# Six changes of order in a gated two-branch encoder layer on one core

## The chip, the cores and the metric

One core of one Trainium2 chip runs the kernel. The metric is the device time of one execution in microseconds (us); lower is better. The median of three runs before the change is 2126.95 us (2126.74 to 2128.09).

## What is computed

The reference is one pre-norm encoder layer in fp32, applied to two inputs with the same weights: x_sample (512 tokens) and x_prompt (1024 tokens), 1024 features each.

```
xn  = rmsnorm(x)
z   = xn @ W_in          # q_A 512 | k_A 128 | v_A 128 | q_B, k_B, v_B 512 each | gate_A, gate_B 1024 each
A   : grouped-query attention, 8 heads of 64 on 2 key groups; q and k RMS-normalised per head,
      then turned by a 2-D rotary table; softmax over all tokens
B   : neighbourhood attention, 8 heads; a band of rows around each block of 128 queries,
      with a relative position bias
mix = (sigmoid(gate_A) * (o_A @ W_pA) + sigmoid(gate_B) * (o_B @ W_pB)) @ W_out
x   = x + mix
x   = x + relu(rmsnorm(x) @ W_up)^2 @ W_down          # 4096 wide
y   = rmsnorm(x)
```

## The kernel before

**Products.** A fp32 product is three matmuls. Every operand is split into a high part, which ScalarE (ACT) casts to fp32r (`split`, L199 for weights), and a remainder, which VectorE (DVE) computes as operand minus high part (L206); TensorE (PE) adds high x high, low x high and high x low into one PSUM bank (`mm3`, L212). So behind each operand stand an ACT cast and a DVE subtraction, and an operand that comes late mostly comes late by its remainder.

**Trunks and phases.** `run` is called once for each input: trunk 0 is x_sample (names with s0, NB = 1 block of 512 tokens), trunk 1 is x_prompt (s1, NB = 2). A last function does the feed-forward part for both. In a trunk, branch A goes by its two key groups g, each with two phases.

Phase R goes over tiles `tt` of 128 tokens. A tile is projected to q and k (`z`) and v; `chain` (L666) squares the heads (ACT, L672), multiplies by the gains (DVE, L676, `ts`), forms the turned pairs `us` with the sine table (GpSimd, POOL, L685), takes the per-head reciprocal root `rs_A` as a power (POOL, L180, in `rstd`), multiplies by the cosine (DVE, L692), adds the pairs (DVE, L693) and scales into `rr` (ACT, L697). Two tiles later `heads_t` transposes `rr` on PE (`pqs`) and empties the bank into kT and qT: high parts on ACT (L626, L628), remainders on DVE (L629, L631); v goes by L653 and L654. In the first group of trunk 1 the rows of x are normalised on the way: `norm_to` (L294) squares a row on ACT (L296), forms mean and power (`ms_s` L176, L180) and the normalised row `xns` (DVE, L300); `transpose_tile` (L305) transposes it on PE (`ptxs`, L313) and empties the bank into the high part (ACT, L323) and the remainder `xs_1l` (DVE, L329).

Phase A goes over heads and blocks of 128 queries: `s_tile` (L777) computes scores `ss` (L785, L786), row maxima (DVE, L788), exponentials (ACT, L791), reciprocals (DVE, L793) and normalised probabilities `ps` (POOL, L794); PE transposes them (`pTs`, L829), ACT and DVE split them (`pths` L834, `ptls` L835), and PE multiplies by v (L805, L806).

Phase B does the neighbourhood attention in units `i` of one head and one query block: scores `sbs`, bias and softmax (L1059 to L1091), transposes `ptbs` (L1132), their split `bhs` (L1139, L1140; in trunk 1 partly through memory and L1122, L1123), the output `obs`. A head pair's projections `pqbs` and `pkbs` are emptied into qB and kB (remainders L1000 and L1021). Near its end the projection of branch A's output starts (`proj_a`, L889): matmuls `ppas` of the split output `oXs` with the split weights `w_pas`, whose splits wait in the list `oa_held`.

**What sets the order.** A scheduler arranges each engine's queue from the order in which the code is written. `tc.keep_in_program_order(op)` holds an instruction at its written place, `tc.issue_after(ins)` puts what is issued inside it behind `ins`. Work that only has to be done some time is held in a generator queue, `fill`, and its pieces are pulled between the steps: the gates (`gate`, L439) in phases R and A, and `proj_a` at the end of phase B, where `f` (L1201 to L1203) is the number of pieces of three matmuls that a unit pulls. `gate` loads the weights of column chunk c + 1 while it works on chunk c, and holds their splits until the third of eight steps:

```
if k == 2:
    while held:
        held.pop(0)()
```

PSUM is held in two pools, one of two double banks for the scores and one of four single banks, which the gate's products (`gpss`), `pTs`, `ptbs`, `ppas` and others take in turn. A gate bank comes free with the tanh (ACT, L460, `sgs`).

## Time and profile before

| | |
|---|---|
| median of 3 runs | 2126.95 us |
| profiled execution | 2126.34 us |
| its span in the profile | 2124.5 us |
| mean granted TensorE clock | 0.999 |
| busy: PE matmuls / weight loads / DVE / ACT / POOL | 2096.5 / 1839.0 / 1480.0 / 1145.7 / 363.3 us |

The profile lists each instruction with its start from the start of the span, its duration, engine, line, operation and tiles (output <- inputs; buffer numbers are left out). Where an engine was idle before an instruction, brackets give the idle time and the instruction that released it. A PE row can overlap the next, as matmuls are pipelined; the pace is read from start to start. SPq and ACTq are queues that issue transfers.

### The profile page before, as it was taken

The numbers are of one execution on the slowest core, as the hardware profiler recorded it, in microseconds if no ns is written. First come the engines' busy times: TensorE is split into PE (matmuls) and PEld (weight loads), VectorE is DVE, ScalarE is ACT, GpSimd is POOL, SyncE is SP. The second block draws the span as 40 slices with busy tenths as digits, with TensorE's granted clock in tenths as the row PEclk, the third lists the DMA queues.
The fourth block names the chain that finished last, engine by engine and source line by source line (L and its number), as shares of the span: only waits on it lengthen the run. The fifth ranks groups of instructions, "written<-read, shape, count | busy, mean of one in ns | idle before, by whom it ended". The sixth has DMA issues, their size and how long they took to land.

```text
span 2124.5 us, 31728 instructions
## 1 busy us (share of the span) xinstructions
PE 2096.5 (99%) x10871; PEld 1839.0 (87%) x10871; DVE 1480.0 (70%) x2793; ACT 1145.7 (54%) x2487; POOL 363.3 (17%) x446
## 2 busy tenths in 40 slices
PE   9999999999999999999999999999999999999998
PEld 8888778888898888887888999999999988888887
DVE  6666786777647756777873877778777777669563
ACT  6665653666666745556531566666565643334452
POOL 2232310332232314443101100002000000000000
PEclk9999999999999999999999999999999999999999
DMA  6436557530122136876563656568454899688561
GB/s 191 133 99 200 160 150 256 192 86 23 49 70 87 45 84 193 241 224 193 172 227 124 199 181 206 163 230 214 156 162 146 272 350 341 213 280 278 164 204 64
DMA packets 336104, 372.92 MB, mean 176 GB/s; under 512 B 31039, under 2 KB 267207, under 8 KB 335943
## 3 DMA queue, kind: packets, MB, share of 16 engines
q1 hardware_dynamic: 297463, 305.60, 45.6%
q10 hardware_dynamic: 31328, 45.11, 6.2%
q0 software_dynamic: 7152, 20.19, 3.5%
q8 instruction: 86, 1.41, 0.3%
q14 instruction: 75, 0.61, 0.1%
HBM read 274.29 MB, written 97.32 MB: 175 GB/s over the span
## 4 chain that ended last, share of the span: by engine, by line
PE 52%; DVE 1%; issue 0%; ACT 0%; POOLq 0%; POOL 0%; ACTq 0%; DVEq 0%
PE dn L212 20%; PE ua L212 6%; PE ud L212 6%; PE uc L212 6%; PE ops L212 4%; PE ub L212 3%; PE ppbs L212 2%; PE ppas L212 2%; PE dnf L212 2%; PE pt L353 1%; PE obs L212 0%; PE ptbs L1132 0%; ACT pbs L1088 0%; PE sbs L212 0%; DVE A L1458 0%
## 5 line engine op out<-in xcount | busy, mean ns | idle before, releaser
L212 PE MATMUL dn<-wd,ah 128*128 128x512 f32 x1248 | 384.2, 389 | 0.0
L212 PEld LDWEIGHTS dn<-wd,ah 128*128 128x128 f32 x1248 | 234.2, 188 | 48.7
L212 PE MATMUL dn<-wd,al 128*128 128x512 f32 x624 | 242.8, 389 | 0.0
L1457 ACT ACTIVATE ah<-ar 128x512 fp32r<-128x512 f32 x168 | 104.4, 627 | 206.7 <-PE dn L212 185.6
L212 PE MATMUL gpss<-xs_0h,w_gs 128*128 128x512 f32 x512 | 189.4, 402 | 0.8 <-DVE ot_Bs L471 0.4
L1458 DVE TENSOR_TENSOR al<-ar,ah 128x512 fp32r<-128x512 f32 x168 | 114.1, 687 | 76.4 <-ACT ah L1457 66.6
L212 PE MATMUL ud<-B,A 128*128 128x384 f32 x768 | 143.7, 334 | 0.7 <-DVE c L1575 0.7
L212 PE MATMUL uc<-B,A 128*128 128x384 f32 x768 | 143.7, 334 | 0.0
L212 PE MATMUL ua<-B,A 128*128 128x384 f32 x768 | 138.8, 334 | 0.0
L212 PEld LDWEIGHTS dn<-wd,al 128*128 128x128 f32 x624 | 117.1, 188 | 24.2
L794 POOL TENSOR_SCALAR ps<-ps,rls 128x1024 f32<-128x1024 f32 (+1 forms) x96 | 96.8, 1009 | 228.4 <-DVE rls L793 213.8
L212 PEld LDWEIGHTS ud<-B,A 128*128 128x128 f32 x768 | 134.0, 188 | 1.1 <-DVE c L1575 1.1
L212 PEld LDWEIGHTS uc<-B,A 128*128 128x128 f32 x768 | 134.1, 188 | 0.2 <-ACT A L1457 0.2
L834 ACT ACTIVATE pths<-pTs 128x512 fp32r<-128x512 f32 x160 | 94.1, 597 | 73.9 <-PE pTs L829 71.3
L212 PEld LDWEIGHTS ua<-B,A 128*128 128x128 f32 x768 | 133.7, 188 | 0.2
L835 DVE TENSOR_TENSOR ptls<-pTs,pths 128x512 fp32r<-128x512 f32 x160 | 107.5, 686 | 37.7 <-ACT pths L834 36.7
L212 PE MATMUL ops<-wh_os,mgs 128*128 128x512 f32 x384 | 119.4, 390 | 0.0
L788 DVE TENSOR_REDUCE nms<-ss 128x1 f32<-128x1024 f32 (+1 forms) x96 | 99.8, 1040 | 25.0 <-PE ss L786 24.5
L212 PEld LDWEIGHTS gpss<-xs_0h,w_gs 128*128 128x128 f32 x512 | 96.1, 188 | 19.0 <-DVE w_gs L206 0.7
L791 ACT ACTIVATE ps<-ss,nms 128x1024 f32<-128x1024 f32 (+1 forms) x96 | 93.3, 972 | 32.1 <-DVE nms L788 26.2
L180 POOL TENSOR_TENSOR rs_f<-ms_f,mhalf 128x1 f32<-128x1 f32 x6 | 4.0, 667 | 590.7 <-DVE ms_f L176 590.7
L829 PEld LDWEIGHTS pTs<-ident,ps 128*128 128x128 f32 x640 | 78.0, 140 | 28.4 <-POOL ps L794 4.4
(287 smaller groups left out, 5144.2 us busy)
## 6 DMA issues: line engine op xcount, KB each, us to landing
ar<-ud SPq DMA_DIRECT2D x120, 512.0 KB, 5.4
br<-in_w_mlp_down_dram SPq DMA_DIRECT2D x72, 512.0 KB, 5.3
rawu<-in_w_mlp_up_dram SPq DMA_DIRECT2D x64, 512.0 KB, 4.1
ud<-c ACTq DMA_DIRECT2D x128, 192.0 KB, 3.6
raw_gs<-in_w_in_dram SPq DMA_DIRECT2D x32, 512.0 KB, 3.9
ud<-cs SPq DMA_DIRECT2D x64, 192.0 KB
tbs<-pbs SPq DMA_DIRECT2D x24, 384.0 KB, 4.8
bhs<-tbs SPq DMA_DIRECT2D x24, 384.0 KB, 3.7
```

Of the source, the lines that this page charges most:

```text
L180: nc.gpsimd.tensor_tensor(r[:, :n], m[:, :n], mhalf[:, :n], op=ALU.pow)
L212: op = nc.tensor.matmul(out, a, b, **kw)
L353: nc.tensor.transpose(halves[c // 4][:, (c % 4) * P : (c % 4 + 1) * P], t[:, c * P : (c + 1) * P], ident)
L788: nc.vector.tensor_reduce(nm_, s, axis=AX.X, op=ALU.max, negate=True)
L791: op = nc.scalar.activation(p, s, AF.Exp, bias=nm_, accum_out=l)
L794: nc.gpsimd.tensor_scalar(p, p, rl, 1.0, op0=ALU.mult, op1=ALU.mult)
L829: nc.tensor.transpose(pt[:, j * P : (j + 1) * P], PP[u, j][:, kc * P : (kc + 1) * P], ident)
L834: nc.scalar.activation(hi, pt, AF.Copy)
L835: nc.vector.tensor_tensor(lo, pt, hi.bitcast(F32), op=ALU.subtract)
L1457: nc.scalar.activation(hi, src, AF.Copy)
L1458: nc.vector.tensor_tensor(lo, src, hi.bitcast(F32), op=ALU.subtract)
```

## The change

All six edits concern order. The number of instructions on each engine is the same.

- `rstd` gets `pow_pin`, and `chain` uses it: the power of the head norms keeps its written place, behind the two multiplications that form the turned pairs.
- `gate`: for chunks after the group's first (c > c0) the splits of the next chunk's weights are issued behind the last exponential that `s_tile` has issued for the first unit (`last_exp`). This concerns chunks 2 (trunk 0, group 0), 6 and 7 (trunk 0, group 1), 2 and 3 (trunk 1, group 0) and 6 and 7 (trunk 1, group 1).
- `next_norm` keeps the written place of the row norms of tiles 6 and 7 of trunk 1.
- In the first phase R of trunk 1, the norm of tile `tr.ready` is written at tile 0 instead of 1, ahead of the carried transposes, and the next one at tile 1 instead of 2.
- At the end of trunk 0's phase B a unit pulls 3 pieces of `proj_a` instead of 3 or 4.
- In trunk 1's phase B the second pop of `oa_held` in a unit starts one unit later (n - 9 instead of n - 10).

```diff
@@ -171,13 +171,15 @@
     def bias_row(r):
         nc.sync.dma_start(biases[r], shifted[:, :, 7 - r : 23 - r, :])
 
-    def rstd(ss, n, width, name, pin=False):
+    def rstd(ss, n, width, name, pin=False, pow_pin=False):
         m = sml.tile([P, 8], F32, tag="ms", name=f"ms_{name}")
         op = nc.vector.tensor_scalar(m[:, :n], ss, 1.0 / width, EPS, op0=ALU.mult, op1=ALU.add)
         if pin:
             tc.keep_in_program_order(op)
         r = sml.tile([P, 8], F32, tag="rs", name=f"rs_{name}")
-        nc.gpsimd.tensor_tensor(r[:, :n], m[:, :n], mhalf[:, :n], op=ALU.pow)
+        op = nc.gpsimd.tensor_tensor(r[:, :n], m[:, :n], mhalf[:, :n], op=ALU.pow)
+        if pow_pin:
+            tc.keep_in_program_order(op)
         return r
 
     held_pe = []
@@ -428,6 +430,7 @@
         obd = dram.tile([4 * P, T], F32, name=f"obd{N}")
         fill = Fill()
         later_put, slot_no = [], [None]
+        last_exp = []
 
         def put(dst, src):
             if slot_no[0] is None:
@@ -453,8 +456,11 @@
                         if k + 1 < NC8:
                             yield
                         if k == 2:
-                            while held:
-                                held.pop(0)()
+                            with ExitStack() as st:
+                                for ins in last_exp if c > c0 else ():
+                                    st.enter_context(tc.issue_after(ins))
+                                while held:
+                                    held.pop(0)()
                     sg = sgp.tile([P, 512], F32, tag="sg", name=f"sg{nm}", bufs=2)
 
                     nc.scalar.activation(sg, g_, AF.Tanh, scale=0.5)
@@ -612,7 +618,7 @@
 
                 def next_norm(tt):
                     xn = ph.tile([P, D], F32, tag="xn", name=f"xn{N}_{tt}", bufs=2)
-                    xn_of[tt] = norm_to(xn, norm_load(x, tt, ph, f"{N}_{tt}"), gb, f"{N}_{tt}")
+                    xn_of[tt] = norm_to(xn, norm_load(x, tt, ph, f"{N}_{tt}"), gb, f"{N}_{tt}", tt > NT // 2 + 1)
 
                 def heads_t(tt):
                     nm = f"{N}_{g}_{tt}"
@@ -688,7 +694,7 @@
                             S4[:, :, :, e].to_broadcast([P, 5, HD // 2]),
                             op=ALU.mult,
                         )
-                    r = rstd(ss[:, :5], 5, HD, f"A{nm}")
+                    r = rstd(ss[:, :5], 5, HD, f"A{nm}", pow_pin=True)
                     nc.vector.tensor_tensor(t, t, rt[:, 0:1, :].to_broadcast([P, 5, HD]), op=ALU.mult)
                     nc.vector.tensor_tensor(t, t, u, op=ALU.add)
                     rr = pre.pop("rr", None) or ph.tile([P, 6, HD], F32, tag="rr", name=f"rr{nm}", bufs=3)
@@ -746,10 +752,9 @@
                             lag.pop(0)()
                     if fresh and not first:
                         if tt == 0:
+                            xn_of[tr.ready] = norm_to(xn_next, xt, gb, f"{N}_{tr.ready}")
                             tr.p0_t(*tr.carry.pop(0))
                         if tt == 1:
-                            xn_of[tr.ready] = norm_to(xn_next, xt, gb, f"{N}_{tr.ready}")
-                        if tt == 2:
                             next_norm(tr.ready + 1)
                     if first and g == 0 and tt == 1:
                         load_pad()
@@ -810,6 +815,7 @@
 
                 for j in range(4):
                     ends = s_tile(units[0], j)
+                    last_exp[:] = [ends]
                     fill.pull(2)
                 queue = []
                 LAG = 2
@@ -1200,7 +1206,7 @@
                 if i < n - 8:
                     f = (5 if i < 2 else 2 + i % 2) if NB == 1 else 5 - (i % 6 == 5)
                 else:
-                    f = 3 + i % 2 if NB == 1 else 8
+                    f = 3 if NB == 1 else 8
                 if NB == 2 and i == n - 11:
                     pa = proj_a(ph, raw_here)
                     next(pa)
@@ -1255,7 +1261,7 @@
                 fill.pull(f - f // 2)
                 for u in due_v.get(i, ()):
                     v_unit(u)
-                if NB == 2 and oa_held and i >= n - 10:
+                if NB == 2 and oa_held and i >= n - 9:
                     oa_held.pop(0)()
                 while later_put and later_put[0][0] < i:
                     nc.sync.dma_start(*later_put.pop(0)[1:])
```

The order of instructions on the engines shows what this moves. Line numbers after the change are 2 to 6 higher than before; names end in the tile's running number.

First, DVE where trunk 0 ends phase R of group 1 (values `vts`, keys `kTs` and queries `qTs` of tile 3, row maxima `nms` and reciprocals `rls` of the first block, `w_gs0_2304_7` the gate weights of chunk 7). Before:

```order
L654 TENSOR_TENSOR vts0_1_3_1624<-zvs0_1_3_1599,vts0_1_3_1624 128x4x64
L206 TENSOR_TENSOR w_gs0_2304_7_1829<-raw_gs0_2304_7_0_1827,w_gs0_2304_7_1829 128x512 x2
L629 TENSOR_TENSOR kTs0_1_1259<-pqs0_1_3_1641,kTs0_1_1259 128x128
L631 TENSOR_TENSOR qTs0_1_0_1257<-pqs0_1_3_1641,qTs0_1_0_1257 64x2x128
L631 TENSOR_TENSOR qTs0_1_1_1258<-pqs0_1_3_1641,qTs0_1_1_1258 64x2x128
L788 TENSOR_REDUCE nms0_1_0_0_0_1671<-ss0_1_0_0_0_1668 128x1
```

After:

```order
L660 TENSOR_TENSOR vts0_1_3_1624<-zvs0_1_3_1599,vts0_1_3_1624 128x4x64
L635 TENSOR_TENSOR kTs0_1_1259<-pqs0_1_3_1641,kTs0_1_1259 128x128
L637 TENSOR_TENSOR qTs0_1_0_1257<-pqs0_1_3_1641,qTs0_1_0_1257 64x2x128
L637 TENSOR_TENSOR qTs0_1_1_1258<-pqs0_1_3_1641,qTs0_1_1_1258 64x2x128
L793 TENSOR_REDUCE nms0_1_0_0_0_1671<-ss0_1_0_0_0_1668 128x1
L798 RECIPROCAL rls0_1_0_0_0_1676<-ls0_1_0_0_0_1674 128x1
L793 TENSOR_REDUCE nms0_1_0_0_1_1691<-ss0_1_0_0_1_1688 128x1
L798 RECIPROCAL rls0_1_0_0_1_1696<-ls0_1_0_0_1_1694 128x1
L793 TENSOR_REDUCE nms0_1_0_0_2_1712<-ss0_1_0_0_2_1709 128x1
L798 RECIPROCAL rls0_1_0_0_2_1717<-ls0_1_0_0_2_1715 128x1
L793 TENSOR_REDUCE nms0_1_0_0_3_1732<-ss0_1_0_0_3_1729 128x1
L208 TENSOR_TENSOR w_gs0_2304_6_1701<-raw_gs0_2304_6_0_1699,w_gs0_2304_6_1701 128x512 x2
```

The two remainders of chunk 7 no longer stand between the values and the keys of tile 3. Those of chunk 6 stand behind the fourth row maximum, those of chunk 7 still further behind.

Second, ACT at the start of phase A of group 1 in trunk 1 (exponentials `ps`, split probabilities `pths`, the gate's tanh `sgs`). Before:

```order
L791 ACTIVATE ps1_1_0_0_3_7890,ls1_1_0_0_3_7891<-ss1_1_0_0_3_7883,nms1_1_0_0_3_7888 128x1024
L791 ACTIVATE ps1_1_0_1_0_7918,ls1_1_0_1_0_7919<-ss1_1_0_1_0_7911,nms1_1_0_1_0_7916 128x1024
L834 ACTIVATE pths1_1_0_0_0_7907<-pTs1_1_0_0_0_7902 128x512
L834 ACTIVATE pths1_1_0_0_1_7932<-pTs1_1_0_0_1_7927 128x512
L460 ACTIVATE sgs1_2304_4_1_7952<-gpss1_2304_4_1_7857 128x512
L791 ACTIVATE ps1_1_0_1_1_7943,ls1_1_0_1_1_7944<-ss1_1_0_1_1_7936,nms1_1_0_1_1_7941 128x1024
```

After:

```order
L796 ACTIVATE ps1_1_0_0_3_7890,ls1_1_0_0_3_7891<-ss1_1_0_0_3_7883,nms1_1_0_0_3_7888 128x1024
L201 ACTIVATE w_gs1_2304_6_7966<-raw_gs1_2304_6_0_7964 128x1024
L201 ACTIVATE w_gs1_2304_7_8426<-raw_gs1_2304_7_0_8424 128x1024
L840 ACTIVATE pths1_1_0_0_0_7907<-pTs1_1_0_0_0_7902 128x512
L796 ACTIVATE ps1_1_0_1_0_7918,ls1_1_0_1_0_7919<-ss1_1_0_1_0_7911,nms1_1_0_1_0_7916 128x1024
L840 ACTIVATE pths1_1_0_0_1_7932<-pTs1_1_0_0_1_7927 128x512
L466 ACTIVATE sgs1_2304_4_1_7952<-gpss1_2304_4_1_7857 128x512
```

Two casts of gate weights, which were made in phase R before, now stand between the fourth exponential of the first block and the first split of its probabilities.

Third, DVE late in phase B of trunk 1 (remainders of attention output `oXs`, projection weights `w_pas`, queries `qBs` and keys `kBs` of the last head pair; L1059, L1100 and L1090 belong to the softmax of a unit). Before:

```order
L206 TENSOR_TENSOR oXs1_0_1_11016<-rawos1_0_1_11014,oXs1_0_1_11016 128x512 x2
L1000 SCALAR_TENSOR_TENSOR qBs1_3_11110<-pqbs1_3_1_11250,qBs1_3_11110 64x128 x4
L1123 TENSOR_TENSOR bhs1_5_2_11211<-bhs1_5_2_11211 128x768
L206 TENSOR_TENSOR w_pas1_0_11010<-raw_pas1_0_0_11008,w_pas1_0_11010 128x256 x2
L1059 ISA sbss1_5_3_0_11222,nmbs1_5_3_0_11223<-sbs1_5_3_11213,bms1_5_3_0_11214 128x384
L1059 ISA nmbs1_5_3_0_11223 128x1
L1059 ISA sbss1_5_3_1_11225,nmbs1_5_3_1_11226<-sbs1_5_3_11213,bms1_5_3_1_11218 128x384
L1059 ISA nmbs1_5_3_1_11226 128x1
L1100 STREAM_TRANSPOSE pbs1_5_0_11098<-pbs1_5_0_11098 128x768
L1090 RECIPROCAL rlbs1_5_3_0_11234<-lbs1_5_3_0_11232 128x1
L1090 RECIPROCAL rlbs1_5_3_1_11239<-lbs1_5_3_1_11237 128x1
L1021 TENSOR_TENSOR kBs1_3_0_11111<-pkbs1_3_1_11285,kBs1_3_0_11111 64x512 x2
```

After:

```order
L1027 TENSOR_TENSOR kBs1_3_1_11112<-pkbs1_3_0_11158,kBs1_3_1_11112 64x512
L208 TENSOR_TENSOR oXs1_0_0_11013<-rawos1_0_0_11011,oXs1_0_0_11013 128x512 x2
L1129 TENSOR_TENSOR bhs1_5_2_11206<-bhs1_5_2_11206 128x768
L1006 SCALAR_TENSOR_TENSOR qBs1_3_11110<-pqbs1_3_1_11245,qBs1_3_11110 64x128 x8
L1027 TENSOR_TENSOR kBs1_3_0_11111<-pkbs1_3_1_11280,kBs1_3_0_11111 64x512 x2
L208 TENSOR_TENSOR w_pas1_0_11010<-raw_pas1_0_0_11008,w_pas1_0_11010 128x256 x2
L208 TENSOR_TENSOR oXs1_0_1_11016<-rawos1_0_1_11014,oXs1_0_1_11016 128x512
L1027 TENSOR_TENSOR kBs1_3_1_11112<-pkbs1_3_1_11280,kBs1_3_1_11112 64x512
L477 TENSOR_TENSOR ot_Bs1_4_3_11338<-obs1_4_3_11331,ot_Bs1_4_3_11338 64x512
```

The keys now follow the queries, ahead of the projection weights and of the second piece of attention output; the softmax rows have moved up, out of this stretch.

## The prediction

> **What bounds the kernel now.** The page comes first. Its first part gives the busy time of each engine, share of the span and number of instructions.
>
> ```profile
> span 2124.5 us, 31728 instructions
> ...
> PE 2096.5 (99%) x10871; PEld 1839.0 (87%) x10871; DVE 1480.0 (70%) x2793; ACT 1145.7 (54%) x2487; POOL 363.3 (17%) x446
> ```
>
> TensorE (PE) works through 2096.5 of 2124.5 us. The change takes no instruction away, so all that it can win lies in the other 28.0 us: the moments in which PE has reached a matmul whose operand or PSUM bank isn't ready. The profiled execution took 2126.34 us, 1.84 more than its span and 0.61 less than the median of 2126.95; I sum against the profiled one and add the result to the median. The second view is the list of waits of PE, each row a matmul that waited, the instruction that released it, the sum, the count and the longest.
>
> ```profile
> PE sbs L212 <- DVE kBs L1021: 2.6, 2, 2.1
> PE zs L212 <- DVE xs_1l L329: 1.5, 1, 1.5
> ...
> PE ss L786 <- DVE kTs L629: 1.3, 2, 1.0
> ...
> PE obs L212 <- DVE bhs L1140: 1.1, 1, 1.1
> PE pTs L829 <- POOL ps L794: 0.8, 3, 0.3
> ...
> PE ptxs L313 <- DVE ms_s L176: 0.5, 1, 0.5
> PE ptxs L313 <- DVE xns L300: 0.5, 1, 0.5
> ```
>
> The reader should see single events, not a rate: one wait for remainders of neighbourhood keys, one for x remainders, two for transposed keys, one for turned-back probabilities. Each of the six edits passes one of these places. How much one costs is read from start to start in the timeline of PE, here where trunk 0 goes from phase R to phase A of group 1.
>
> ```profile
> 128.40 0.39 PE L212 MATMUL gpss<-xs_0l,w_gs 128*128 128x512 f32 x1
> 128.62 0.39 PE L212 MATMUL gpss<-xs_0h,w_gs 128*128 128x512 f32 x1
> 129.45 0.50 PE L785 MATMUL ss<-kTs,qTs 128*128 128x512 f32 x1 [0.44 <-DVE vts L654]
> 130.91 0.50 PE L786 MATMUL ss<-kTs,qTs 128*128 128x512 f32 x1 [0.96 <-DVE kTs L629]
> ```
>
> Undisturbed, one 128x512 matmul follows another after 0.22 to 0.23 us (128.40 to 128.62). The two score matmuls start 0.83 and 1.46 us after the one before, so they lose 0.60 and 1.23, while the listed waits are 0.44 and 0.96: an interruption costs some 0.16 to 0.27 more than the idle time in brackets, because the pipeline fills again. I add 0.17 to every wait that vanishes.
>
> **Gate weights, trunk 0.** VectorE (DVE) at the same place:
>
> ```profile
> 129.37 1.28 DVE L206 TENSOR_TENSOR w_gs<-raw_gs,w_gs 128x512 fp32r<-128x512 f32 x2
> 130.57 0.28 DVE L629 TENSOR_TENSOR kTs<-pqs,kTs 128x128 fp32r<-128x128 f32 x1
> ```
>
> The last key remainder stands behind two remainders of gate weights, 1.28 us, which nobody needs for a long time. The changed order takes both away (the first pair of rows from the order), and with them the remainder of the chunk before, a few rows ahead. The key remainder then ends not at 130.85 but 1.28 + 0.64 sooner, at about 128.9, when PE would ask for it at 129.08, and the value remainder ahead of it comes sooner too. Gain 0.60 + 1.23 = 1.8. The splits return between the first exponentials and their row sums, where I charge 0.2.
>
> **Gate weights, trunk 1.** In group 0 the second of the two kTs waits (1.3 - 0.96 = 0.34, with the refill 0.5) goes in the same way; group 1 has no such wait. But both groups pay. These are ScalarE (ACT) behind the fourth exponential of group 1, the mean of one cast of gate weights, and PE at the same moment:
>
> ```profile
> 655.82 0.19 ACT L791 ACTIVATION_READ_ACCUMULATOR ps<-ss,nms 128x1 f32 x1
> 657.36 1.11 ACT L791 ACTIVATE ps<-ss,nms 128x1024 f32<-128x1024 f32 x1 [1.35 <-DVE nms L788]
> ...
> 658.47 1.07 ACT L834 ACTIVATE pths<-pTs 128x512 fp32r<-128x512 f32 x2
> 659.42 0.61 ACT L460 ACTIVATE sgs<-gpss 128x512 f32<-128x512 f32 x1
> ```
>
> ```profile
> L199 ACT ACTIVATE w_gs<-raw_gs 128x1024 fp32r<-128x1024 f32 x32 | 33.6, 1063 | 4.1 <-DMA raw_gs<-in_w_in_dram 2.5 <-issue 1.4
> ```
>
> ```profile
> 659.23 0.60 PE L829 MATMUL pTs<-ident,ps 128*128 128x128 f32 x4
> ...
> 660.35 0.40 PE L212 MATMUL gpss<-xs_0h,w_gs 128*128 128x512 f32 x1
> ```
>
> Two casts (2 x 1.06 = 2.1 at most, 2.0 with the overlap) now fill the 1.35 us of idle time from 656.0 and end near 658.0. Two pths casts (0.95 from start to start of the tanh), an exponential (1.1) and then the tanh that empties the gate's bank follow in ACT's queue: the tanh starts near 660.05 instead of 659.42 and ends near 660.65. The next gate matmul needs that bank. It started at 660.35, behind three score matmuls (3 x 0.23 = 0.69) that the new order of PE puts after it: PE asks at about 659.66. New wait 660.65 - 659.66, about 0.9 to 1.0; I take 0.9 in each group. Bounds: 0, if the exponential's own input comes late enough that nothing is in front of the tanh, and both casts in full, 2.1, in each group. I take 0.9 as the rows around it give every term of it. Net for trunk 1: -0.5 + 1.8 = +1.3.
>
> **Norms one tile sooner, powers behind turned pairs.** DVE and GpSimd (POOL) in phase R of trunk 1:
>
> ```profile
> 407.29 1.28 DVE L300 SCALAR_TENSOR_TENSOR xns<-xts,rs_s,gbs 128x1024 f32<-128x1024 f32 x1 [1.16 <-POOL rs_s L180]
> ...
> 408.90 1.28 DVE L329 TENSOR_TENSOR xs_1l<-ptxs,xs_1h 128x512 fp32r<-128x512 f32 x2
> ...
> 413.84 0.49 DVE L676 TENSOR_TENSOR ts<-zs,gtab 128x320 f32<-128x320 f32 x1
> ...
> 416.21 0.49 DVE L692 TENSOR_TENSOR ts<-ts,rts 128x320 f32<-128x320 f32 x1 [1.75 <-POOL us L685]
> ```
>
> ```profile
> 413.88 1.18 POOL L180 TENSOR_TENSOR rs_As<-ms_As,mhalf 128x5 f32<-128x5 f32 x1 [3.01 <-DVE ms_As L176]
> 415.02 1.16 POOL L685 TENSOR_TENSOR us<-ts,rts 128x160 f32<-128x160 f32 x2
> ```
>
> Up to 408.5 DVE is held by a row norm (1.16 idle for its power, then 1.28 of work) that belongs to the tile after the one PE waits for: the 1.5 us wait for xs_1l. With both row norms asked for one tile sooner this norm is done before, and tile 4's own (the 0.5 wait on xns) is too. The 0.5 wait listed under ms_s is for a PSUM bank that the x remainders free; they stand behind L692 at 416.21, which waits for the turned pairs, which wait for a power of 1.18 us. With the power behind them the pairs can start when L676 ends, near 414.33, and L692 some 0.7 us sooner at the least. The power is needed only after the sum behind L692, so it moves into cover. Gain 1.5 + 0.5 + 0.5 + 3 x 0.17 = 3.0, of which I leave 0.3 because a 128x1024 norm step of 1.28 us now lies in tiles 0 and 1 instead: 2.7. Pinning the norms of tiles 6 and 7 and the powers of trunk 0 I cost at nothing; PE shows no wait there that ends on them.
>
> **Key remainders ahead of projection weights.** PE and DVE late in phase B of trunk 1:
>
> ```profile
> 975.19 0.34 PE L212 MATMUL sbs<-kBs,qBs 128*128 128x384 f32 x1
> 977.65 0.81 PE L212 MATMUL sbs<-kBs,qBs 128*128 128x384 f32 x3 [2.12 <-DVE kBs L1021]
> ...
> 986.62 0.39 PE L212 MATMUL ppas<-oXs,w_pas 128*128 128x512 f32 x1
> ```
>
> ```profile
> 973.09 0.76 DVE L206 TENSOR_TENSOR w_pas<-raw_pas,w_pas 128x256 fp32r<-128x256 f32 x2 [1.57 <-ACT w_pas L199]
> ...
> 976.23 1.36 DVE L1021 TENSOR_TENSOR kBs<-pkbs,kBs 64x512 fp32r<-64x512 f32 x2
> ```
>
> DVE sits idle for 1.57 us for a cast of projection weights that nothing needs before 986.62, works it off, passes a softmax tile, and only then writes the keys that PE asked for at 975.37. In the new order the keys stand ahead of the weights and the softmax tile before both. Put at 973.09 or sooner, the pair of 1.36 ends by 974.45, 0.9 before PE asks. Gain 2.12 + 0.17 = 2.3. The weights and the attention output that are moved back have from 976 to 986.62; that is the cover, and beyond it their delay would be a wait one to one.
>
> **Fewer fillers per unit at the end of trunk 0's phase B.** PE and DVE:
>
> ```profile
> 309.68 0.38 PE L1132 MATMUL ptbs<-ident,pbs 128*128 128x128 f32 x2
> 309.81 0.48 PE L212 MATMUL obs<-bhs,vss 128*128 128x256 f32 x2
> ```
>
> ```profile
> 310.92 0.42 DVE L1140 TENSOR_TENSOR bhs<-ptbs,bhs 128x256 fp32r<-128x256 f32 x1
> ```
>
> The last transposes start at 309.68 and their remainder is there at 311.34, 1.66 us on; only one pair of matmuls lies between, so the last output matmul waits the listed 1.1. The new order leaves nine projection matmuls (9 x 0.23 = 2.0) between these transposes and that pair and nine more behind it, so 1.66 is covered. Gain 1.1 + 0.17 = 1.3. Every transpose moves up too, by at most fifteen matmuls (3.4 us); if its probabilities were not ready then, that much could come back, but no row of the list shows PE waiting for them near here. The load of the next projection weights moves behind two other loads on the SP queue; its cover is the rest of the phase.
>
> **A rule against the change.** The gate remainders read two SBUF operands, and they move to where POOL normalises the probabilities:
>
> ```profile
> 470.64 0.67 DVE L206 TENSOR_TENSOR wgls<-rawqs,wghs 128x512 fp32r<-128x512 f32 x1
> ```
>
> ```profile
> 470.81 1.49 POOL L794 TENSOR_SCALAR ps<-ps,rls 128x1024 f32<-128x1024 f32 x1 [0.70 <-DVE rls L793]
> ```
>
> ```profile
> L794 POOL TENSOR_SCALAR ps<-ps,rls x96: 691/1120/1508, 54.7 to 759.0; 128x1024 f32<-128x1024 f32 x64, 128x512 f32<-128x512 f32 x32
> ```
>
> The last row has shortest, median and longest in ns; 64 of the 96 are of this size. A normaliser that starts 0.50 us before such a remainder ends took 1.49, 0.37 over the median. The Trainium skill (SBUF — State Buffer, section "SBUF: two separate sides") says that VectorE, when it reads two SBUF inputs, and GpSimd lock a shared port pair for a whole instruction, and the later one blocks; the trace agrees, with 0.37 of the 0.50. By that rule the sum would be the second rival below.
>
> **The sum.** -1.8 + 0.2 (trunk 0) + 1.3 (trunk 1, gates) - 2.7 - 2.3 - 1.3 = -6.6. On the profiled time that is 2119.7, on the median 2120.3. The likeliest case's own range: without any of the new waits -8.9 (with the 0.3 back), so 2118.0; with 2.1 instead of 0.9 in both groups -4.2, so 2122.7.
>
> **Rivals.** A measurement of this kernel tells about 0.2%, 4.25 us, from no change, so up to 2122.7 is faster.
>
> First, waits handed on: the queue is as long as before, and the next instruction is late instead. The norm step of 1.28 then holds up a tile's eviction in tile 0 or 1, giving the 1.67 of the xs_1l wait back, and the displaced projection weights reach 986.62 late and give back the 2.3. That is -6.6 + 1.67 + 2.3 = -2.6, 2124.3: no change. For it: ACT and DVE lose no work. Against: both have idle time around these places (1.16 and 1.57 in the rows).
>
> Second, the port: each of the 14 moved remainders (three chunks in trunk 0, four in trunk 1, two each) meets a normaliser: 14 x 0.37 = 5.2, thus -1.4, 2125.5. Against it, three waits of PE on the normaliser sum to 0.8 in the whole list, so they are mostly covered.
>
> Third, slower: phase A runs at the pace of the chain from reduction through exponential and normaliser to transposes, and what is put into it lengthens it one to one. Seven casts at 1.06 and 14 remainders at 0.64 (half of 1.28) are 7.4 + 9.0 = 16.4 in place of the 2.0 charged: -6.6 - 2.0 + 16.4 = +7.8, 2134.8. It decides from the point where ACT or DVE has no room left. Phase A of group 1 in trunk 1, with length and busy time of PE, PEld, DVE, ACT and POOL:
>
> ```profile
> 655.00:700.00 45.00, 44.91 (x246) 36.81 (x246) 32.71 (x53) 32.20 (x57) 16.00 (x14) 1.00 0.11 32
> ```
>
> Against: 12 of 45 us are free on both, and two casts and four remainders need 2.1 and 2.6.
>
> **Chances.** The forecast 0.78; handed on 0.11; port 0.06; slower 0.05. So faster 0.78, same 0.17, slower 0.05. The time is 2120.3. The range takes in the likeliest case and the first rival: 2117.6, a little under its lower end as 0.17 per interruption may be 0.2, to 2124.4.
>
> **What would show it.** Right: the rows kBs L1021 (its 2.1), xs_1l, bhs L1140 and both kTs leave the list of PE's waits, and new ones on the tanh (sgs L460 in the old numbers) of some 0.7 appear at the starts of phase A in trunk 1. Wrong: new rows on oXs or w_pas near 985, on normalised probabilities in phase A, on qTs or kTs in tiles 0 to 2 of trunk 1, or more transposes of ptbs waiting before 310. If PE's busy time or clock changes, the argument is about the wrong thing.

## The result and the profile after

The changed kernel takes 2116.49 us (2115.74 to 2118.62, 6 runs), the kernel before on the same chip 2126.82 us (6 runs): ratio 0.9952, 95% interval 0.9939 to 0.9965, so 10.3 us less (7.4 to 13.0). The forecast was 6.6 less, and its range ended at 2117.6, 1.1 us short of what came. That margin is small: timed again (below, "The change again") the same program took 2118.26 us, 8.7 less than before (6.4 to 11.7), which lies inside the range. So what was wrong is read from the single stretches rather than from the total. The profiled execution took 2116.56 us. The first lines of its page, to be held against those of before:

```profile
span 2114.6 us, 31728 instructions
...
PE 2092.2 (99%) x10871; PEld 1838.6 (87%) x10871; DVE 1478.7 (70%) x2793; ACT 1146.4 (54%) x2487; POOL 361.8 (17%) x446
```

The same instructions, the same work on DVE, ACT and POOL: what is gone is waiting. PE's busy time fell as well, by 4.3 of the 9.9 us by which the span is shorter, which the prediction had named as a sign of being wrong. Here it isn't one: the matmuls are the same and the mean granted clock is 0.999 in both, but a matmul behind an interruption is recorded as longer (0.50 us at 130.91 before, 0.39 now), and 1.0 of the 4.3 is the start of the kernel, which no edit touches. The list of waits of PE in the changed kernel, the rows that answer to those of before (columns: matmul and line, releaser, sum, count, longest; lines are those of the changed kernel, 2 to 10 higher):

```profile
PE zs L214 <- DVE xs_1l L331: 1.2, 1, 1.2
PE ppas L214 <- DVE ot_Bs L477: 1.1, 1, 1.1
...
PE ppbs L214 <- ACT oXs L485: 0.5, 1, 0.5
PE sbs L214 <- DVE kBs L1027: 0.5, 1, 0.5
...
PE pTs L835 <- POOL ps L799: 0.3, 1, 0.3
...
PE pTs L835 <- DVE ptls L841: 0.2, 1, 0.2
```

The long wait for kBs (2.1) and those for kTs, bhs, tile 4's xns and the bank behind ms_s have left the list, as forecast. The wait for xs_1l has not: 1.2 of 1.5 is still there. Two rows of some size are new: ppas behind ot_Bs, 1.1, and ppbs behind oXs, 0.5. No row on the tanh (sgs) stands at a start of phase A; the forecast wanted one in each group of trunk 1. The place that the prediction read first, PE at the start of phase A of trunk 0's second group, now looks so:

```profile
126.54 0.39 PE L214 MATMUL gpss<-xs_0h,w_gs 128*128 128x512 f32 x1
126.77 0.39 PE L790 MATMUL ss<-kTs,qTs 128*128 128x512 f32 x1
126.99 0.39 PE L791 MATMUL ss<-kTs,qTs 128*128 128x512 f32 x1
```

0.22 to 0.23 us from start to start: both interruptions are gone.

**Where the time went.** Every kernel here issues the same 10871 matmuls, so the time between the starts of two of them, counted in order of start, compares one stretch of work across kernels (inside a stretch the order of the products can differ). The columns are single profiled executions: before, after, the changed program profiled a second time (again), and three kernels that have one part of the change each (described below).

| matmuls | what lies there | before | after | again | gates | powers | norms |
|---|---|---|---|---|---|---|---|
| 0 to 50 | start of the kernel | 12.22 | 11.35 | 12.22 | 11.78 | 11.42 | 11.35 |
| 200 to 700 | trunk 0, group 0, R to A | 85.54 | 84.79 | 84.77 | 84.75 | 85.13 | 85.53 |
| 700 to 825 | trunk 0, group 1, R to A | 27.77 | 25.11 | 25.11 | 25.11 | 26.11 | 27.72 |
| 1475 to 1640 | trunk 0, end of phase B | 34.36 | 33.43 | 33.66 | 34.40 | 34.31 | 34.31 |
| 1990 to 2050 | trunk 1, tiles 0 and 1 | 9.12 | 8.47 | 8.45 | 10.12 | 8.44 | 8.73 |
| 2050 to 2150 | trunk 1, xs_1l | 16.13 | 15.62 | 15.02 | 15.89 | 17.67 | 17.75 |
| 2150 to 2390 | trunk 1, group 0, R to A | 35.88 | 34.94 | 34.93 | 34.94 | 34.94 | 35.14 |
| 2390 to 2530 | start of phase A, group 0 | 28.27 | 27.56 | 27.56 | 27.55 | 28.25 | 28.27 |
| 3550 to 3650 | start of phase A, group 1 | 18.67 | 18.66 | 18.65 | 18.68 | 18.65 | 18.65 |
| 5000 to 5250 | keys in trunk 1's phase B | 55.24 | 53.51 | 53.50 | 55.82 | 54.95 | 54.93 |

After less before: -0.87, -0.75, -2.66, -0.93, -0.65, -0.51, -0.94, -0.71, -0.01 and -1.73, together -9.76 of the 9.9 by which the span is shorter. The first of these is none of the change's: no edit touches the start, and the same program took 12.22 there the second time. Three of the entries are marked by the clock and not by an edit: 55.82 (gates), 17.67 (powers) and 17.75 (norms) each hold 3.41 us at half the granted clock; see the norms alone.

### The profile page after: what moved, and what is told of

Same layout as the page of the kernel before. It is cut to its first block, busy times and chain, and to the rows that moved or that the text cites. A ratio compares the mean times of both kernels' runs of the same rounds, so it can differ in the third digit from the quotient of the medians.

```text
span 2114.6 us, 31728 instructions
## 1 busy us (share of the span) xinstructions
PE 2092.2 (99%) x10871; PEld 1838.6 (87%) x10871; DVE 1478.7 (70%) x2793; ACT 1146.4 (54%) x2487; POOL 361.8 (17%) x446
## 4 chain that ended last, share of the span: by engine, by line
PE 78%; DVE 1%; issue 1%; ACT 0%; POOL 0%; DMA 0%; POOLq 0%; DVEq 0%; ACTq 0%
PE dn L214 20%; PE gpss L214 8%; PE ud L214 6%; PE ua L214 6%; PE uc L214 6%; PE ops L214 3%; PE ub L214 3%; PE pTs L835 3%; PE zs L214 2%; PE ppbs L214 2%; PE pqbs L214 2%; PE pkbs L214 2%; PE ppas L214 2%; PE zvs L214 2%; PE dnf L214 2%; PE os L811 1%
## 5 line engine op out<-in xcount | busy, mean ns | idle before, releaser
L799 POOL TENSOR_SCALAR ps<-ps,rls 128x1024 f32<-128x1024 f32 (+1 forms) x96 | 97.4, 1016 | 227.6 <-DVE rls L798 209.6
```

The source lines that it names most:

```text
L799: nc.gpsimd.tensor_scalar(p, p, rl, 1.0, op0=ALU.mult, op1=ALU.mult)
```

## The experiments

Each kernel was timed beside the kernel before on the same chip.

**One part of the change alone: the gates.** The kernel before with this edit (and `last_exp`, which it needs):

```diff
                         if k == 2:
-                            while held:
-                                held.pop(0)()
+                            with ExitStack() as st:
+                                for ins in last_exp if c > c0 else ():
+                                    st.enter_context(tc.issue_after(ins))
+                                while held:
+                                    held.pop(0)()
```

> The kernel before with the edit of the gate weights alone. Theory now: the splits cost PE nothing where they return, because the gate's next products don't take the bank that the delayed tanh empties; the gains at the ends of phase R stay: about -0.4 and -2.2 in trunk 0, -1.0 to -1.6 in trunk 1, together about -4, near 2123. Rival, the step of the prediction: a new wait of 0.9 at the start of phase A in each group of trunk 1, so -1.6 + 1.3 = -0.3, near 2126.5.

Measured: 2121.53 us (2120.01 to 2124.46, 11 runs) beside 2126.67, ratio 0.9975 (0.9966 to 0.9984), 5.1 us less. All of trunk 0's gain ahead of phase B is there (-0.79 and -2.66), trunk 1's start of phase A is 0.72 shorter in group 0 and unchanged in group 1. So the edit that was charged +1.3 in trunk 1 costs nothing there.

**All but the gates.** The changed kernel with the lines above undone:

```diff
-                            with ExitStack() as st:
-                                for ins in last_exp if c > c0 else ():
-                                    st.enter_context(tc.issue_after(ins))
-                                while held:
-                                    held.pop(0)()
+                            while held:
+                                held.pop(0)()
```

> All edits but that of the gate weights. Theory now: the rest of the change is worth what is left of it, about -6, near 2121, in the stages where its edits act, and the stalls at the ends of phase R (group 1 of trunk 0, group 0 of trunk 1) are back with 1.8 and 0.7 us. Rival: the gates are worth next to nothing, as the prediction's sum has it, and this kernel runs like the whole change, near 2117.

Measured: 2121.15 us (2119.16 to 2121.81, 7 runs), ratio 0.9972 (0.9961 to 0.9983), 5.5 us less than before. Its stretch 700 to 825 takes 26.15 and 2150 to 2390 takes 34.91: something other than the gates removes 1.6 of the first and all of the second. The 0.7 at the start of phase A of group 0 is the gates' own: without them 2390 to 2530 takes 28.23.

**The powers alone.** The kernel before with

```diff
-                    r = rstd(ss[:, :5], 5, HD, f"A{nm}")
+                    r = rstd(ss[:, :5], 5, HD, f"A{nm}", pow_pin=True)
```

> The kernel before with the power of the head norms in its written place alone. Theory: the 0.7 us at the transposes of tile 6 in phase R of trunk 1 go, and in trunk 0 some 0.4 us at the heads of group 1: -0.5 to -1.2, near 2126. Rival: a power that waits behind the pairs makes the scaled heads late, 0.5 us or more slower.

Measured: 2123.08 us (2122.22 to 2123.91, 10 runs) beside 2127.3, ratio 0.9982 (0.9973 to 0.9991), 4.2 us less, several times what was expected. PE and DVE of this kernel in trunk 0, group 1:

```profile
127.97 0.50 PE L788 MATMUL ss<-kTs,qTs 128*128 128x512 f32 x1 [0.47 <-DVE kTs L631]
```

```profile
126.09 0.42 DVE L656 TENSOR_TENSOR vts<-zvs,vts 128x256 fp32r<-128x256 f32 x1
126.43 1.28 DVE L208 TENSOR_TENSOR w_gs<-raw_gs,w_gs 128x512 fp32r<-128x512 f32 x2
127.63 0.28 DVE L631 TENSOR_TENSOR kTs<-pqs,kTs 128x128 fp32r<-128x128 f32 x1
```

The gate remainders still stand in front of the last keys. But the turned pairs no longer stand behind a power on GpSimd, so DVE is through the tiles ahead sooner and comes to these rows sooner: its sum (L693 before, L695 here) for the last tile starts at 121.51 instead of 124.44, 2.9 us sooner, while PE is only 1.3 us ahead there. The wait of 0.96 is 0.47 and that of 0.44 is gone. The powers of trunk 0, costed at nothing, are worth 1.66 and 0.41 there. In trunk 1 they take away the same 0.94 from 2150 to 2390 as the gates do, and the wait of 0.54 for the bank behind ms_s; but the norm still stands in front of the remainder of x, and the wait for xs_1l is 2.19 us instead of 1.5.

**The norms alone.** The kernel before with

```diff
                         if tt == 0:
+                            xn_of[tr.ready] = norm_to(xn_next, xt, gb, f"{N}_{tr.ready}")
                             tr.p0_t(*tr.carry.pop(0))
                         if tt == 1:
-                            xn_of[tr.ready] = norm_to(xn_next, xt, gb, f"{N}_{tr.ready}")
-                        if tt == 2:
                             next_norm(tr.ready + 1)
```

and the pinned norms of tiles 6 and 7.

> The kernel before with the two edits of the row norms alone (one tile sooner, tiles 6 and 7 in their written place). Theory now: the row norm of tile 4 now asks for its x row when the load has hardly landed, and the remainders of tile 4 still stand behind the product with the cosine, so most of the 2.3 us expected does not come: 0 to -1.0, 2125.7 to 2126.7, with waits of ScalarE on the x row and a wait of PE of about 1.3 for the remainders left. Rival, the prediction's step: both waits go, -2.0, near 2124.7.

Measured: 2126.28 us (2125.61 to 2127.52, 10 runs), ratio 0.9997 (0.9988 to 1.0006): nothing that stands clear of the noise. The norm is out of the way, and the remainder now stands behind the product with the cosine, which waits for the pairs; DVE and PE of this kernel:

```profile
408.15 0.49 DVE L692 TENSOR_TENSOR ts<-ts,rts 128x320 f32<-128x320 f32 x1 [1.80 <-POOL us L685]
408.56 0.68 DVE L329 TENSOR_TENSOR xs_1l<-ptxs,xs_1h 128x512 fp32r<-128x512 f32 x1
```

```profile
409.30 0.44 PE L212 MATMUL zs<-wghs,xs_1l 128*128 128x384 f32 x1 [2.20 <-DVE xs_1l L329]
```

With powers or norms alone the stretch 2050 to 2150 is 1.5 to 1.6 longer than before (17.67, 17.75), more than the stretch ahead of it gains (0.4 to 0.7); with both it is 0.5 to 1.1 shorter. The wait itself is only 0.7 longer than before (2.19 and 2.20 against 1.50). The rest is the clock: in both profiles the granted clock of TensorE falls to 0.50 for 3.41 us, 0.8 to 0.9 us behind the end of this wait: from 407.44 us with the powers alone and from 410.12 with the norms alone. The first row gives a window of the kernel with the powers alone (us), its length, PE's busy time and matmuls, the granted clock, and the DMA engines' share and GB/s; the others are PE in it:

```profile
407.50:410.80 3.30, 3.30 (x15) 0.50 0.33 122
```

```profile
409.16 0.52 PE L214 MATMUL zs<-wghs,xs_1h 128*128 128x384 f32 x1
409.48 0.52 PE L214 MATMUL zs<-wgls,xs_1h 128*128 128x384 f32 x1
```

These products start 0.32 us apart, and 0.17 to 0.18 at full clock. Half of 3.41 us, some 1.7, is lost (an estimate); without that both stretches would be near 16.0, as long as before, as the 0.7 lost at xs_1l is won back at the bank behind ms_s. In the changed kernel the longest of these waits is 1.19, and its profile shows no such stretch of half clock. The profile of the gates alone has one too, from 974.78 us behind a wait of 1.84 for kBs. It doesn't follow every time: the kernel before waits 2.12 for kBs, and the one with the cosine behind the remainders 2.02 for a bank, at full clock. What decides, and how many of the other executions have it, no trace here shows.

**The two edits of phase B alone.** The kernel before with

```diff
-                    f = 3 + i % 2 if NB == 1 else 8
+                    f = 3 if NB == 1 else 8
...
-                if NB == 2 and oa_held and i >= n - 10:
+                if NB == 2 and oa_held and i >= n - 9:
```

> The kernel before with the two edits of phase B alone (3 pieces per unit in trunk 0, second pop one unit later in trunk 1). Theory: -0.9 at the end of trunk 0's phase B, where the first product with branch B's output now waits 0.5 to 0.65 us for its last piece, and -1.7 in trunk 1, where 2.4 us go and up to 0.9 come back because the remainders of the second projection weights run beside the bias masks on GpSimd (0.8 and 1.1 us instead of 0.42 each): -2.6, near 2124.1. Rival, the prediction's steps: -3.6, near 2123.1, with neither of the new waits.

Measured: 2124.22 us (2123.46 to 2125.42, 10 runs), ratio 0.9988 (0.9979 to 0.9997), 3.1 us less; 53.52 for 5000 to 5250 and 33.90 for 1475 to 1640. The four parts alone are worth 5.1 + 4.2 + 1.0 + 3.1 = 13.4, all together 10.3 or, in the next run, 8.7: they overlap. The table shows where: from 700 to 825 gates and powers take away 2.66 and 1.66 alone and 2.66 together, and from 2150 to 2390 gates, powers and norms take away 0.94, 0.94 and 0.74 alone and 0.94 together.

**The change again**, the same program, for the spread of a profile.

> The whole change once more, unaltered, beside the next two kernels. If its time is a property of the program: 2116.5 within 1 us again, with the first 50 matmuls over after 11.4 us and matmuls 1990 to 2050 in 8.5. If the two places drift from execution to execution, as the 11.35 to 12.2 and 8.4 to 10.3 of the other kernels allow: up to 2118.5, with either place longer.

Measured: 2118.26 us (2117.40 to 2119.89, 5 runs) beside 2126.97, ratio 0.9958 (0.9945 to 0.9970), 8.7 us less. Over both, 11 runs from 2115.74 to 2119.89. The stretches of the table agree within 0.1 us but for the start (12.22 against 11.35), 1475 to 1640 (33.66 against 33.43) and 2050 to 2150 (15.02 against 15.62).

**The tanh later still.** The changed kernel with four casts of 128x512, into a tile that nothing reads, behind the fourth exponential in both groups of trunk 1, to see how much room ACT has before a late tanh costs something:

```diff
                     last_exp[:] = [ends]
+                    if NB == 2 and j == 3:
+                        idle = ph.tile([P, 512], F32, tag="idle", name=f"idle{N}_{g}", bufs=1)
+                        for _ in range(4):
+                            tc.keep_in_program_order(nc.scalar.activation(idle, xh(0, 0), AF.Copy))
                     fill.pull(2)
```

> The whole change, with four casts of 128x512 more (0.5 us each, into a buffer that nobody reads) on ScalarE behind the fourth exponential of each group of trunk 1, so that the tanh starts 2 us or more later than in the whole change. Theory: ScalarE has only about 0.2 us left there, and PE waits 1 to 2 us in each group at the first matmul that takes the tanh's bank or the probabilities behind it, not at the gate's products: +2 to +4 us, near 2119.5. Rival: ScalarE has room for all of it, no new wait of PE over 0.3, near 2116.5.

Measured: 2118.17 us (2117.98 to 2118.95, 4 runs), ratio 0.9960 (0.9947 to 0.9974), as without the casts; the starts of phase A take 27.60 and 18.66 us. First ACT and PE of the changed kernel at the start of phase A of group 1:

```profile
647.82 0.19 ACT L796 ACTIVATION_READ_ACCUMULATOR ps<-ss,nms 128x1 f32 x1
647.91 1.99 ACT L201 ACTIVATE w_gs<-raw_gs 128x1024 fp32r<-128x1024 f32 x2
...
651.97 0.61 ACT L466 ACTIVATE sgs<-gpss 128x512 f32<-128x512 f32 x1
```

```profile
651.22 0.60 PE L835 MATMUL pTs<-ident,ps 128*128 128x128 f32 x4
651.58 0.47 PE L214 MATMUL gpss<-xs_0h,w_gs 128*128 128x512 f32 x1
```

Then the same of the kernel with the casts:

```profile
649.25 0.19 ACT L796 ACTIVATION_READ_ACCUMULATOR ps<-ss,nms 128x1 f32 x1
...
655.53 0.61 ACT L466 ACTIVATE sgs<-gpss 128x512 f32<-128x512 f32 x1
```

```profile
652.65 0.60 PE L839 MATMUL pTs<-ident,ps 128*128 128x128 f32 x4
653.00 0.48 PE L214 MATMUL gpss<-xs_0h,w_gs 128*128 128x512 f32 x1
```

The tanh now starts 6.28 us after the row sum of the fourth exponential (649.25 to 655.53) instead of 4.15 (647.82 to 651.97), and the next chunk's first gate matmul starts 2.53 us ahead of it. So that matmul does not need the bank which the tanh empties. The theory that 0.2 us of room was left falls; ACT has more than 2 us. The trace of the kernel before had it already, if not at the place that the prediction read: of the 47 times that one gate product follows another, the next one starts ahead of the tanh that empties the last one's bank in 21. One of them lies 11 us ahead of that place (PE and ACT of the kernel before):

```profile
648.82 0.39 PE L212 MATMUL gpss<-xs_1h,w_gs 128*128 128x512 f32 x1
```

```profile
649.11 0.59 ACT L460 ACTIVATE sgs<-gpss 128x512 f32<-128x512 f32 x1
```

**The cosine apart.** The changed kernel, in which VectorE needn't wait for the pairs before the product, as this goes into another tile:

```diff
-                    nc.vector.tensor_tensor(t, t, rt[:, 0:1, :].to_broadcast([P, 5, HD]), op=ALU.mult)
-                    nc.vector.tensor_tensor(t, t, u, op=ALU.add)
                     rr = pre.pop("rr", None) or ph.tile([P, 6, HD], F32, tag="rr", name=f"rr{nm}", bufs=3)
+                    tc_ = rr[:, :5, :]
+                    nc.vector.tensor_tensor(tc_, t, rt[:, 0:1, :].to_broadcast([P, 5, HD]), op=ALU.mult)
+                    nc.vector.tensor_tensor(t, tc_, u, op=ALU.add)
```

> The whole change, and the product with the cosine is written into the buffer that the scaled heads take later, not over its own input. Theory: the x remainders that PE still waits 1.2 us for in phase R of trunk 1 stand on VectorE behind that product, and it waits for GpSimd only because it overwrites what GpSimd reads; with another buffer the wait shrinks to 0.3 or less and the time falls by 1 to 1.5 us, near 2115.3. Rival: the remainders are late by their own cast on ScalarE or by the row norm, the wait stays at 1.2 and the time at 2116.5.

Measured: 2118.37 us (2117.71 to 2119.17, 5 runs), ratio 0.9961 (0.9948 to 0.9973). PE of this kernel:

```profile
404.19 0.44 PE L214 MATMUL zs<-wghs,xs_1l 128*128 128x384 f32 x1 [0.61 <-DVE xs_1l L331]
405.81 1.06 PE L315 MATMUL ptxs<-ident,xns 128*128 128x128 f32 x8 [1.00 <-DVE ms_s L176]
```

The wait for xs_1l goes from 1.19 to 0.61, and 1.00 appears at the transposes of the next tile, which wait for the bank that the second remainder frees (by the order on DVE; the row names ms_s, right behind it). 15.58 us for the stretch against 15.62: handed on.

**The cosine behind the remainders.** The changed kernel with that product (and what hangs on it) written, and held, behind the x remainders, for tile 2 of trunk 1 alone:

```diff
+                    def rest(pin=False):
-                    nc.vector.tensor_tensor(t, t, rt[:, 0:1, :].to_broadcast([P, 5, HD]), op=ALU.mult)
+                        op = nc.vector.tensor_tensor(t, t, rt[:, 0:1, :].to_broadcast([P, 5, HD]), op=ALU.mult)
+                        if pin:
+                            tc.keep_in_program_order(op)
...
+                    if fresh and not first and tt == NT // 2 - 2:
+                        rests.append(rest)
+                    else:
+                        rest()
...
                         next_tile()
+                        while rests:
+                            rests.pop(0)(True)
```

> The changed kernel, with the product of tile 2's heads with the cosine (and the sum and scaling behind it) written behind the x remainders of tile 4 in the first phase R of trunk 1, and held there. Nothing else moves on VectorE, and the first transposes of tile 5 stand five matmuls sooner on TensorE. My theory: the 1.19 us wait for xs_1l that the change left behind is there only because the remainder stands behind a product that waits 1.20 us for GpSimd's turned pairs. With the remainder ahead, both are done 0.7 us after their casts, near 402.4 on the clock of the profiled run, and the wait goes (1.19 and 0.17 of refill); tile 5's transposes then ask near 401.9 for the bank that the second remainder frees near 402.4, and give back some 0.5 to 0.7. So the stretch of 100 matmuls goes from 15.6 us to 14.8 or 15.0, and the whole to 0.7 us under the changed kernel's, 2116 to 2117.5. Rival, waits handed on: VectorE then stands still for the power of tile 6's norm, whose own queue place on GpSimd is behind the same turned pairs, the product of tile 2 comes 2 us later, and the turned heads of tile 2 or the values behind it keep TensorE waiting: the stretch stays at 15.6 or more, or the stretch behind it grows beyond 34.94 by as much. Second rival: what an undisturbed run shows there is the landing of the rows, and the stretch in front grows by what this one loses.

Measured: 2119.74 us (2117.30 to 2122.35, 6 runs) beside 2126.61, ratio 0.9967 (0.9954 to 0.9979). First DVE and PE of the changed kernel:

```profile
402.29 0.49 DVE L698 TENSOR_TENSOR ts<-ts,rts 128x320 f32<-128x320 f32 x1 [1.20 <-POOL us L691]
402.70 0.68 DVE L331 TENSOR_TENSOR xs_1l<-ptxs,xs_1h 128x512 fp32r<-128x512 f32 x1
```

```profile
403.43 0.44 PE L214 MATMUL zs<-wghs,xs_1l 128*128 128x384 f32 x1 [1.19 <-DVE xs_1l L331]
```

Then DVE and PE of this kernel:

```profile
401.75 1.28 DVE L331 TENSOR_TENSOR xs_1l<-ptxs,xs_1h 128x512 fp32r<-128x512 f32 x2
402.95 0.14 DVE L176 TENSOR_SCALAR ms_s<-sss 128x1 f32<-128x1 f32 x1
404.69 1.29 DVE L302 SCALAR_TENSOR_TENSOR xns<-xts,rs_s,gbs 128x1024 f32<-128x1024 f32 x1 [1.60 <-POOL rs_s L180]
405.89 0.49 DVE L699 TENSOR_TENSOR ts<-ts,rts 128x320 f32<-128x320 f32 x1
...
409.19 0.17 DVE L176 TENSOR_SCALAR ms_As<-ssAs 128x5 f32<-128x5 f32 x1 [1.00 <-ACT sqs L678]
```

```profile
413.46 1.06 PE L315 MATMUL ptxs<-ident,xns 128*128 128x128 f32 x8 [2.02 <-DVE ms_s L176]
```

The remainders follow one another with no idle time ahead of them, and the wait for xs_1l is gone, as the theory had it. But the product comes 4.14 us after the first remainder starts (401.75 to 405.89) instead of ahead of it, ACT's scaling and then its squares of the next tile come late with it (the 1.00 before ms_As), and the transposes of tile 6 wait 2.02 for a bank. The stretch takes 15.71: the rival was right, and the whole wait turned up one tile later. (This profile also took 271.22 us between matmuls 3650 and 5000, late in phase B, against 268.97 in the changed kernel's; the edit doesn't touch that.)

**The x row loaded first.** The changed kernel with the row of x for tile 4 issued on SP ahead of the first gate weights and the gains:

```diff
-            nxt_w = load_cols(win, goff + c0 * P, P, f"g{N}_{goff}_{c0}")
+            with ExitStack() as st:
+                for ins in x_load if goff == 2304 and c0 == 0 else ():
+                    st.enter_context(tc.issue_after(ins))
+                nxt_w = load_cols(win, goff + c0 * P, P, f"g{N}_{goff}_{c0}")
...
+                    xt = ph.tile([P, D], F32, tag="xt", name=f"xt{N}_{tr.ready}", bufs=2)
+                    x_load.append(nc.sync.dma_start(xt, x[tr.ready * P : (tr.ready + 1) * P, :]).ins)
                     gb = ph.tile([P, 1, D], F32, tag="gb", name=f"gb{N}", bufs=1)
...
-                    xt = norm_load(x, tr.ready, ph, f"{N}_{tr.ready}")
```

> The whole change, and on the SP queue the load of the x row of trunk 1's tile 4 and of the norm's gains no longer stands behind the load of the first gate weights, which waits there for a free buffer. Theory: since the norm was moved a tile sooner, phase R of trunk 1 starts on the landing of that row (8.6 to 10.9 us after its issue in the runs so far); issued sooner, the waits of ScalarE on the row and of GpSimd on the rotary rows go, and matmuls 1990 to 2050 take 8.4 to 8.5 us instead of 8.5 to 10.1: 0 to 1 us faster than the whole change, 2115.5 to 2116.5, in step with its best runs. Rival: the landing is set by the traffic and not by the issue, the time stays within 0.5 us of the whole change or goes up.

Measured: 2118.46 us (2117.40 to 2119.46, 5 runs), ratio 0.9962 (0.9948 to 0.9975). 1990 to 2150 takes 23.53 us, against 24.10 and 23.47 in the two profiles of the changed kernel: no gain that its own drift doesn't give.

**Projection weights later.** The changed kernel with the split of the second projection weights held until the first block's product is through:

```diff
+                    late = [] if NB == 2 and c == 0 else None
                     nxt_w = load_cols(
-                        w["w_proj_a"][0], (c + 1) * P, P, f"pa{N}_{c + 1}", slot_left, raw_of=raw_of
+                        w["w_proj_a"][0], (c + 1) * P, P, f"pa{N}_{c + 1}", slot_left, hold=late, raw_of=raw_of
                     )
...
+                    while late:
+                        late.pop(0)()
                     yield
```

> The whole change, and the split of the second projection weights in trunk 1's phase B is made behind the first block's product instead of ahead of it. Theory: the 1.1 us that PE waits for there come from those two remainders, slowed to 0.8 and 1.1 us beside GpSimd's bias masks, which stand ahead of the output remainder that frees PE's bank; with them behind it the wait falls to 0.3 or less, matmuls 5000 to 5250 take about 52.5 us instead of 53.5, and the time is 1 us lower than that of the whole change. Rival: the bank is freed late by ScalarE or the output itself, and the wait stays.

Measured: 2118.54 us (2117.03 to 2119.07, 5 runs), ratio 0.9958 (0.9945 to 0.9970), the change's own 2118.26 beside it. The weights are out of the way, and the wait stays, 1.03; ACT, DVE and PE of this kernel:

```profile
979.96 0.98 ACT L1097 ACTIVATE pbs<-sbss,nmbs 128x384 f32<-128x384 f32 x1
...
980.97 0.59 ACT L476 ACTIVATE ot_Bs<-obs 64x512 f32<-64x512 f32 x1
```

```profile
981.60 0.68 DVE L477 TENSOR_TENSOR ot_Bs<-obs,ot_Bs 64x512 f32<-64x512 f32 x1 [0.45 <-ACT ot_Bs L476]
```

```profile
982.34 0.50 PE L214 MATMUL ppas<-oXs,w_pas 128*128 128x512 f32 x1 [1.03 <-DVE ot_Bs L477]
```

DVE is idle for 0.45 there; the cast stands behind exponentials on ACT. The matmul has its operands; it waits for the PSUM bank of obs, which this cast and remainder empty. The theory, that the weights' remainders on DVE alone make it late, falls: with them gone, ACT's queue does.

**Both together** (the two edits above).

> That kernel, with the x row and the norm's gains loaded ahead of the first gate weights as well. Theory: the two gains add, matmuls 1990 to 2150 in 23.5 and 5000 to 5250 in 52.5, 1.0 to 1.6 us below the whole change. Rival: with the load moved the time goes back up to about 2118, as in the kernel with that edit alone, for a reason outside these two stages.

Measured: 2117.54 us (2116.94 to 2119.19, 5 runs), ratio 0.9956 (0.9942 to 0.9970). The interval of the changed kernel beside it, 0.9945 to 0.9970, holds this: no version here is shown to beat the change.

## Why the prediction was wrong

The sign, most of the places and most of the mechanisms were right; the sum was 3.7 us too small by the medians and 3.3 by the profiles (9.9 against 6.6). Part of what looks right is luck: the gates and trunk 0 came out 4.8 us better than forecast, the norms, keys and fillers 2.5 worse, and these errors partly cancel; 0.9 is drift. By steps, forecast and measured stretch:

- **Gates in trunk 1: +1.3, measured -1.66 (-0.94, -0.71, -0.01). This is the step that failed: "The next gate matmul needs that bank."** The delay of the tanh was forecast well: 4.23 us behind the fourth row sum (655.82 to 660.05), measured 4.15. But the gate matmul that follows starts at 651.58, ahead of that tanh, and 2.53 us ahead of it with the extra casts. The 0.9 in each group was a wait without a row: no tanh stood in the list of waits at these places, and that a pool of four banks is shared doesn't say which bank comes next. Nothing took its place, so the +1.8 was pure error. The gain of 0.5 was 0.94, since the score matmul ahead of the listed wait was late too: 0.46 after its predecessor, at 453.18, where no wait is listed. This gain isn't the gates' alone: the powers alone bring the same 0.94 and the norms alone 0.74. The -0.71 is below.
- **Trunk 0: -1.6, measured -3.41 (-0.75 and -2.66).** The two interruptions went as worked out (0.60 and 1.23 from start to start). The rest lay where no term stood. Just ahead, the three transposes of the last heads took 0.72 us to the next matmul before (126.00 to 126.72) and take 0.25 now (124.36 to 124.61). The powers, costed at nothing, take 1.66 and 0.41 off the two stretches when alone; with the gates the second stretch is no shorter than with the gates alone (25.11), so it is the same stall that both remove. And the gates change the order of PE as well: the first transposes of probabilities stand two matmuls later, and a normaliser that was late is less so. PE of the kernel before:

```profile
138.89 0.40 PE L785 MATMUL ss<-kTs,qTs 128*128 128x512 f32 x1
139.54 0.33 PE L829 MATMUL pTs<-ident,ps 128*128 128x128 f32 x1 [0.26 <-POOL ps L794]
```

 and of the changed kernel:

```profile
134.82 0.40 PE L790 MATMUL ss<-kTs,qTs 128*128 128x512 f32 x1
135.05 0.39 PE L791 MATMUL ss<-kTs,qTs 128*128 128x512 f32 x1
135.28 0.40 PE L214 MATMUL gpss<-xs_0h,w_gs 128*128 128x512 f32 x1
135.81 0.33 PE L835 MATMUL pTs<-ident,ps 128*128 128x128 f32 x1
```

 The 0.65 from the score matmul to the transpose was 0.42 too long; 0.53 is left from 135.28 to 135.81, so 0.12 is gained here. Another 0.24 goes just behind, where four transposes took 0.60 us to the next matmul (140.63 to 141.23) and now take 0.35 (136.45 to 136.80). The same happens in group 0. With 0.60, 1.23 and the 0.47 of the three transposes that makes 2.66. In the list such waits fall from three (0.8) to one (0.3). In trunk 1, group 0, the wait of a transpose for ptls goes in the same way, with the gates alone too, and with it most of the 0.71. The charge of 0.2 for the splits' return is not to be seen.
- **Norms and powers in trunk 1: -2.7, measured -1.16, -1.79 again.** The xs_1l wait was to vanish and shrank from 1.5 to 1.2 (0.58 in the second profile). "This norm is done before" is right; but the product L698 took its place in front of the remainder, with a wait of 1.20 for the pairs. That is the first rival, waits handed on, at a place it didn't name, and two experiments that pushed the wait further show the same: it turned up as 1.00 or 2.02 at the transposes of the next tiles. How large this term is can't be said closer than 1 us: in the three kernels without an edit there (before, gates, phase B) the two stretches take 25.26, 26.02 and 26.17, and with all of the change's edits there and none besides (after, again, all but the gates, tanh later, weights later) 24.10, 23.47, 25.45, 24.71 and 24.46.
- **Keys: -2.3, measured -1.73.** The wait of 2.12 went, at its price of 2.3 (powers and norms alone have it with 1.83 and 1.84, so -1.4 against these). Then 0.9 came back: a projection matmul waits for the bank of obs, whose remainder ot_Bs now stands behind the displaced weights on DVE and, as the kernel with these later shows, behind exponentials on ACT. So a wait for a bank was charged where there is none and not looked for where there is one.
- **Fillers: -1.3, measured -0.93 and -0.70.** The wait for bhs went as forecast; the matmuls that it had held up now reach the next operand oXs 0.48 early, and up to 1.03 in the other kernels with this edit.
- **Drift: 0, measured -0.87**, the start of the kernel.

The rival of the port clash was priced at 5.2 and is not there: PE's wait for the normalisers fell from 0.8 to 0.3, and their mean time rose only from 1009 to 1016 ns. The slower one is refuted by the unchanged starts of phase A, with four more casts in each.

What stays open: why single runs of this program differ by 4 us (2115.74 to 2119.89), beyond the stretches named; which bank the gate's product takes, as no row names one; and when a long wait is followed by half the clock.

## What to carry to other kernels

A new wait may be charged only where a row shows that consumer waiting for that releaser, or where the trace shows the two in that order everywhere; a shared pool of banks is no such row, and comparing the consumer's start with the releaser's, not at the one place but at all 47 of the trace, would have told it. Edits that empty the same queue ahead of the same deadline don't add, and those that hand a wait to each other can be worth little apart in that place and something together (norms and powers): price them in the combinations that ship. Before a stretch that has grown is explained by order, read its granted clock: a wait of some 2 us was followed here by half the clock in three profiles, which cost more than the part by which the wait had grown. A wait of PE on one engine often starts two queues further back, so before moving its releaser forward look at what then stands last in that queue, and at the tile after.
